# One row maximum per component and a fixed bank order in differential-attention scores

## The chip, the cores and the metric

The kernel runs on one core of a Trainium2 chip. The metric is device time in microseconds (us), the median over runs. The core's engines run side by side, each with its own instruction stream in a fixed order, and wait for each other through semaphores: PE (TensorE, matmuls and transposes; PEld is its weight load), DVE (VectorE), ACT (ScalarE), POOL (GpSimd) and SP (SyncE), which issues the DMA transfers. PE writes its results to PSUM, which has eight banks of 512 float32 columns on each of 128 partitions.

## What is computed

One layer of a hybrid block over 1024 latent tokens and 256 context tokens, width 1024. A modulated RMSNorm and one wide input projection feed two branches, a gated linear attention and a differential attention; each passes its own projection, they are merged through sigmoid gates, and one output projection follows. The change lies in the differential attention. Each of its 8 heads has two components, with one softmax each over 256 + 1024 keys:

```python
def one_block(qs):
    qb1, qb2 = qs
    s1 = jnp.einsum('bhqd,bhkd->bhqk', qb1, k1).astype(jnp.float32) * scale
    s2 = jnp.einsum('bhqd,bhkd->bhqk', qb2, k2).astype(jnp.float32) * scale
    a = jax.nn.softmax(s1, axis=-1) - lam * jax.nn.softmax(s2, axis=-1)
    return jnp.einsum('bhqk,bhkv->bhqv', a.astype(v.dtype), v)
```

## The kernel before

The program has a first part (norms, projections, gated linear attention), the attention stretch, and a last part (branch and output projections). The attention works in 64 units, one for each head and block of 128 queries.

In a unit the scores of both components, 2 x 1280 columns, fill one PSUM tile `s5` of five banks (0 to 4). Component 0 has columns 0 to 1279, component 1 columns 1280 to 2559, so both share bank 2: the last 256 columns of component 0 (its tail) and the first 256 of component 1 (its tail). `att_scores` issues for component 0 four matmuls of 512 columns (two key chunks, each with two accumulating halves), then the four tail matmuls of both components, then the four of component 1. `att_max` takes three negated row maxima on DVE: over component 0's 1024 columns, over both tails at once (128 x 2), over component 1's 1024. `att_exp` combines a component's maximum with its tail's by a small DVE minimum, and takes the exponential of all 1280 columns on ACT with that bias and a running sum. `att_mix` forms the difference of the two softmaxes (up to a factor) on DVE. `att_tr` transposes it in ten pieces on PE, `att_split` splits each into two float32r parts on ACT, POOL and DVE, `att_av` multiplies by the values for two units together, and `att_fin` normalises and stores the result.

Three counters, `s0`, `s1` and `st`, guard the scores: `s0` and `s1` a component's main columns, given back after its exponential; `st` both tails, given back after the second exponential of the unit. `banked` adds the semaphore waits between engines that use the same bank, in whichever direction they are issued, and takes away those between different banks. `att_keys` loads the keys of a head into slots of the tile `hk`, three of them (tag `kk`), two for each head; a head's event `ev_k` is set when both of its components are there, and both slots are given back after the head's last scores.

PE has other work to do in between: `fill` computes gate projections (kind 0) and the branch projections (kinds 1 and 2) in half tiles of 24 matmuls, at the lowest priority. While the scores' PSUM pools are open these write the tile `mb`, afterwards one of five tiles `mc`. When a kind ends, its input buffers `h0` and `h1` are loaded anew (`h<-d_aT`, `h<-d_bT`).

The order of all instructions is made when the program is built: `Driver` keeps a planned time for each engine (`op`, with `LAT` as the delay from one engine to the next), tasks are generators that yield the event or planned time they wait for, and the due task with the best priority goes next. `Driver.key` says which pieces of a tile count as one in that plan. So a change in one task can move every other task's instructions.

Of the kernel before, what the change touches and what calls it, by code (L numbers as in the profile page):

```python
# [11 lines left out]
F32R = mybir.dt.float32r  # L12
BF16 = mybir.dt.bfloat16
AF = mybir.ActivationFunctionType
ALU = mybir.AluOpType
# [5 lines left out]
P = 128  # L21
# [3 lines left out]
T = S + CTX  # L25
# [33 lines left out]
class Driver:  # L59
# [43 lines left out]
    def op(self, eng, cost, outs, ins):  # L103

        t = self.now if eng == "PE" else self.free[eng]
        shared = list(outs) + [x for x in ins if x.space == PSUM]
        for x in ins:
            t = max(t, self.ready.get(self.key(x), 0.0))
        for x in shared:

            end, by = self.last.get(self.key(x), (0.0, eng))
            t = max(t, end if by == eng else end + self.LAT[by])
        for x in outs:
            if eng != "PE":
# [6 lines left out]
        for x in ins + list(outs):  # L121
# [107 lines left out]
class Hybrid:  # L229
# [1 line left out]
    TAGS = dict(  # L231
        h0=("sb", 16), h1=("sb", 16), raw=("sb", 3), sm=("sb", 48),

        hk=("sbK", 1), hc=("sbK", 16), kk=("sbK", 3),

        w=("sbA", 18), p=("sbA", 5), pl=("sbA", 4), rope=("sbA", 1),

# [8 lines left out]
        e5=("sbB", 6), at4=("sbB", 6), at2=("sbB", 2), ac=("sbB", 2), b1k=("sbB", 5), fin=(None, 2),  # L246
# [4 lines left out]
        mb=("psW", 1), s0=("psB", 1), s1=("psB", 1), st=("psB", 1), s5=("psB", 1), b1=("psB1", 2), mc=("psC", 5), mz=("psD", 2),  # L251
# [93 lines left out]
    def banked(self, ins, eng, *banks):  # L345


        seen, info = set(), mybir.DependencyInfo(mybir.DependencyClass.Sync, mybir.DependencyReason.DATA)
        for prev, by, on in reversed(self.recent):
            if by == eng:  # L350
                continue
            if on.isdisjoint(banks):
                self.tc.declare_no_dep(ins, prev, reason="other banks")
            elif by not in seen:
                seen.add(by)
                self.tc.add_manual_dep(ins, prev.name, info, reason="the same bank")
        self.recent = self.recent[-48:] + [(ins, eng, set(banks))]
# [1369 lines left out]
    def att_keys(self):  # L1727

        for hd in range(8):
            c, x = hd // 4, hd % 4  # L1730
            for i in range(10):
                yield self.ev_st["dk", c, i]
            if hd:
                yield self.ev_q[0, 1]
            else:
                yield self.gla_free[3]
                yield from self.acq("hc", 16)
                Driver.places = (T, 2 * T, 3 * T)
                self.hk = self.t("hk", [P, HK], F32R)
            K = []  # L1740
            for comp in range(2):
                rows = slice(64 * comp, 64 * comp + 64)
                yield from self.acq("kk")
                m = (2 * hd + comp) % 3
                kt = self.hk[:, m * T:(m + 1) * T]
                self.dma(kt[0:64], self.d_kT[0][c][x, rows])
                self.dma(kt[64:128], self.d_kT[1][c][x, rows])
                K.append(kt)
            self.K[hd] = K
            self.d.set(self.ev_k[hd], self.d.when(*K))  # L1750

    def att_queries(self):
        yield self.ev_b2
# [30 lines left out]
    def att_scores(self):  # L1784

        nc, d = self.nc, self.d
        yield self.ev_b
        s5 = self.t("s5", [P, 2 * T])
        for hd in range(8):
            for qt in range(8):  # L1790
                pr, qs = qt // 2, slice((qt % 2) * P, (qt % 2) * P + P)
                yield self.ev_k[hd]
                yield self.ev_q[hd, pr]
                K, Q = self.K[hd], self.Q[hd, pr]

                def score(po, comp, o, n):
                    bank = po.offset % (2 * T) // 512
                    for j in range(2):
                        e = self.mm(po, Q[comp][:, j, qs], K[comp][:, o:o + n], j == 0, j == 1)
                        self.banked(self.ins, "PE", bank)  # L1800
                    return e

                u = dict(hd=hd, qt=qt, E=[None, None], mt=self.t("sm", [P, 2]), mx=[self.t("sm", [P, 1]) for _ in range(2)],
                         z=self.t("sm", [P, 2]), left=2, ev=[Event() for _ in range(3)])

                for comp in range(2):
                    yield from self.acq(f"s{comp}")
                    pm = s5[:, 1536 * comp:1536 * comp + 1024]
                    for x, (o, n) in enumerate(self.MAIN[comp]):
                        e = score(pm[:, x * 512:(x + 1) * 512], comp, o, n)  # L1810
                        if x == 0:
                            yield AtPE(0)
                    d.spawn(self.att_max(u["ev"][comp], u["mx"][comp], pm, 3 * comp, 3 * comp + 1), On(e, "DVE"), prio=-3)
                    yield AtPE(0)
                    if comp == 0:
                        yield from self.acq("st")
# [4 lines left out]
                    elif qt == 7:  # L1821
                        self.rel("kk", e, 2)
# [6 lines left out]
    def att_max(self, ev, mx, pm, *banks):  # L1829
        self.dve.tensor_reduce(mx, pm, AX.X, ALU.max, negate=True)  # L1830
        self.banked(self.dve.ins, "DVE", *banks)
        self.d.set(ev)
        return
        yield

    def att_exp(self, u, comp, s5):
        d, mx = self.d, u["mx"][comp]
# [7 lines left out]
        e = self.act.activation(E, s5[:, 1280 * comp:1280 * comp + T], AF.Exp, bias=mx, accum_out=u["z"][:, comp:comp + 1])  # L1845
        self.banked(self.act.ins, "ACT", *range(2 * comp, 2 * comp + 3))
        self.rel(f"s{comp}", e)
        u["left"] -= 1
        if u["left"] == 0:
            self.rel("st", e)  # L1850
# [318 lines left out]
    def phase_b(self):  # L2169
        d = self.d  # L2170
# [14 lines left out]
            d.set(self.ev_b)  # L2185

        d.spawn(to_b(), prio=-3)
        self.ev_k, self.ev_v = [Event() for _ in range(8)], [Event() for _ in range(8)]
# [34 lines left out]
    def phase_c(self):  # L2223
        a, d = self.a, self.d
# [4 lines left out]

        def to_c():  # L2230
            yield self.ev_s2
            yield from self.idle("s0", "s1", "st")
            self.close("psB")
            self.open("psC")
            d.set(self.ev_c)
# [228 lines left out]
```

## Time and profile before

| | |
|---|---|
| runs | 1683.67, 1685.21, 1689.54 us; median 1685.21 |
| profiled execution, first to last instruction | 1685.9 us |
| DVE, ACT, POOL busy | 69%, 47%, 36% of the span |
| DMA moved | 302.84 MB, mean 180 GB/s |

The page lists of the profiled execution only the span; the runs are other executions of the same program. A group's row reads: line, engine, operation, tiles (out<-in), shapes and count, then busy us, mean ns of one, and the engine's idle time before these with what ended it. A row of busy times by stretch reads: start and end, length, then for PE, PEld, DVE, ACT and POOL the busy us with the count in brackets, then granted clock, DMA share and GB/s. All compute instructions stand at a line of a helper, so groups are told apart by their tiles: `s` is the score tile, `sm` small statistics, `e` the exponentials, `at` the split transposes, `b` the two banks for transposes and value products, `mb` and `mc` the fill.

### The profile page before, as it was taken

The numbers are of one execution on the slowest core, as the hardware profiler recorded it, in microseconds if no ns is written. First come the engines' busy times: TensorE is split into PE (matmuls) and PEld (weight loads), VectorE is DVE, ScalarE is ACT, GpSimd is POOL, SyncE is SP. The second block draws the span as 40 slices with busy tenths as digits, with TensorE's granted clock in tenths as the row PEclk, the third lists the DMA queues.
The fourth block names the chain that finished last, engine by engine and source line by source line (L and its number), as shares of the span: only waits on it lengthen the run. The fifth ranks groups of instructions, "written<-read, shape, count | busy, mean of one in ns | idle before, by whom it ended". The sixth has DMA issues, their size and how long they took to land.

```text
span 1685.9 us, 24403 instructions
## 1 busy us (share of the span) xinstructions
PE 1641.8 (97%) x8389; PEld 1358.3 (81%) x8389; DVE 1167.5 (69%) x2035; ACT 788.4 (47%) x1624; POOL 601.7 (36%) x649
## 2 busy tenths in 40 slices
PE   8999999999999999999999999999999999999999
PEld 3788788888788888888878888888888787887887
DVE  4797853455578697687762988787787887525694
ACT  4666423343334535455442665556666555411231
POOL 1500200000156475465530446555565555700000
PEclk9999999999999999999999999999999999999999
DMA  8557947687683665645375344345368552279422
GB/s 305 167 205 258 325 164 248 226 282 273 200 258 114 197 203 169 207 134 169 117 196 154 85 128 132 104 116 138 113 169 245 167 157 67 98 234 337 151 100 75
DMA packets 255884, 302.84 MB, mean 180 GB/s; under 512 B 21480, under 2 KB 173968, under 8 KB 255760
## 3 DMA queue, kind: packets, MB, share of 16 engines
q1 hardware_dynamic: 255760, 301.29, 56.9%
q8 instruction: 66, 1.08, 0.3%
q14 instruction: 58, 0.48, 0.1%
HBM read 203.71 MB, written 97.52 MB: 179 GB/s over the span
## 4 chain that ended last, share of the span: by engine, by line
PE 43%; DVE 6%; ACT 2%; DMA 2%; POOL 2%; issue 2%; ACTq 0%; DVEq 0%; POOLq 0%; SPq 0%
PE mc L335 10%; PE mm L335 7%; PE mb L335 7%; PE s L335 6%; PE b L335 5%; DVE sm L197 3%; PE b L361 3%; POOL at L197 2%; DVE e L197 2%; PE go L335 1%; ACT e L197 1%; DMA h<-d_bT 1%; PE mz L335 1%; PE gs L335 1%; PE tp L361 1%
## 5 line engine op out<-in xcount | busy, mean ns | idle before, releaser
L335 PE MATMUL mm<-w,h 128*128 128x512 f32 x1260 | 319.3, 402 | 0.6 <-DVE w L197 0.4
L335 PEld LDWEIGHTS mm<-w,h 128*128 128x128 f32 x1260 | 232.0, 189 | 48.0 <-issue 1.0
L197 DVE TENSOR_REDUCE sm<-s 128x1 f32<-128x1024 f32 (+1 forms) x192 | 194.4, 1037 | 49.0 <-PE s L335 47.4
L335 PE MATMUL mb<-h,wt 128*128 128x512 f32 x744 | 204.5, 407 | 2.5 <-ACT ft L197 2.1
L197 ACT ACTIVATE e<-s,sm 128x1280 f32<-128x1280 f32 x128 | 169.9, 1330 | 68.0 <-DVE sm L197 60.3
L197 POOL TENSOR_TENSOR at<-ac,at 128x512 fp32r<-128x512 f32 x128 | 184.7, 1443 | 10.7
L197 POOL TENSOR_SCALAR at<-ac 128x512 fp32r<-128x512 f32 x128 | 100.6, 786 | 236.0 <-ACT ac L197 166.9
L335 PE MATMUL s<-hk,aq 128*128 128x512 f32 (+1 forms) x768 | 178.2, 365 | 3.2 <-ACT e L197 1.1
L335 PEld LDWEIGHTS mb<-h,wt 128*128 128x128 f32 x744 | 131.1, 190 | 25.9 <-ACT ft L197 3.6
L335 PE MATMUL mc<-h,wt 128*128 128x512 f32 x600 | 141.2, 392 | 1.7 <-DMA h<-d_bT 0.8
L335 PE MATMUL mm<-h,w 128*128 128x512 f32 x576 | 139.4, 398 | 2.7 <-ACT p L197 1.1
L335 PEld LDWEIGHTS s<-hk,aq 128*128 128x128 f32 x768 | 122.3, 190 | 23.9 <-ACT e L197 5.1
L335 PEld LDWEIGHTS mc<-h,wt 128*128 128x128 f32 x600 | 111.3, 188 | 26.9 <-DMA h<-d_bT 3.3
L335 PE MATMUL b<-at,vv 128*128 128x256 f32 x960 | 130.6, 285 | 0.5 <-POOL at L197 0.4
L335 PEld LDWEIGHTS mm<-h,w 128*128 128x128 f32 x576 | 108.6, 191 | 27.0 <-DVE h L197 1.4
L335 PEld LDWEIGHTS b<-at,vv 128*128 128x128 f32 x960 | 122.7, 190 | 5.6 <-POOL at L197 1.2
L197 POOL TENSOR_TENSOR sm<-sm,nhalf 128x2 f32<-128x2 f32 (+2 forms) x94 | 106.1, 1129 | 53.6 <-DVE sm L197 48.1
L197 DVE TENSOR_TENSOR w<-raw,w 128x512 fp32r<-128x512 f32 x120 | 92.5, 789 | 31.5 <-ACT w L197 30.3
L197 ACT ACTIVATE ac<-b 128x512 f32<-128x512 f32 x120 | 71.1, 600 | 84.9 <-PE b L361 79.7
L197 DVE SCALAR_TENSOR_TENSOR e<-e,sm,e 128x1280 f32<-128x1280 f32 x64 | 108.7, 1698 | 0.6
L197 ACT ACTIVATE w<-raw 128x512 fp32r<-128x512 f32 x120 | 72.5, 628 | 70.3 <-DVE raw L197 22.8
L361 PE MATMUL b<-ident,e 128*128 128x128 f32 x598 | 92.5, 276 | 12.4 <-DVE at L197 4.3
(283 smaller groups left out, 2832.5 us busy)
## 6 DMA issues: line engine op xcount, KB each, us to landing
raw<-in_w_in SPq DMA_DIRECT2D x63, 512.0 KB, 4.7
g<-d_s SPq DMA_DIRECT2D x32, 640.0 KB, 5.2
aq<-d_qT SPq DMA_DIRECT2D x128, 128.0 KB, 3.4
d_dv<-pl SPq DMA_DIRECT2D x40, 256.0 KB, 2.2
gv<-d_v SPq DMA_DIRECT2D x40, 256.0 KB, 3.2
d_kT<-pl SPq DMA_DIRECT2D x40, 256.0 KB, 3.0
hk<-d_kT SPq DMA_DIRECT2D x32, 320.0 KB, 5.7
vv<-d_dv SPq DMA_DIRECT2D x16, 640.0 KB, 6.2
```

Of the source, the lines that this page charges most:

```text
L197: self.ins = f(out, *args, **kw).ins
L335: self.ins = self.nc.tensor.matmul(out, lhsT, rhs, start=start, stop=stop, skip_group_check=more).ins
L361: self.nc.tensor.transpose(out, src, self.ident[:n, :n])
```

## The change

`att_max` goes. Per component there is one maximum over its 1280 columns, in `att_exp`. The tail of component 0 is issued ahead of its main columns, the tail of component 1 behind its own and only after the first maximum. Two gates per unit fix the order on bank 2: the first exponential is issued after the second tail, the second exponential after the next unit's first tail. The counter `st` is gone. `banked` no longer adds waits between ACT and DVE. The plan's `op` treats the score banks one by one, and in them makes PE follow ACT and DVE, and ACT and DVE follow PE, but not each other. Keys have a fourth slot, a tile of its own (`kx`), and an event for each component.

```diff
@@ Driver
-        if x.name.startswith("s5"):
-            o = ap.offset % (2 * T) if ap is not x else 0
-            return x.name + ("t" if ap.free_size() <= 512 and o // 512 == 2 else "ab"[o >= 1280])
+    @staticmethod
+    def banks(ap):
+        x = getattr(ap, "tensor", ap)
+        if not x.name.startswith("s5"):
+            return ()
+        o = ap.offset % (2 * T) if ap is not x else 0
+        return [f"{x.name}b{b}" for b in range(o // 512, (o + ap.free_size() - 1) // 512 + 1)]
@@ Driver.op
+        scores = [b for x in list(outs) + list(ins) for b in self.banks(x)]
+        if scores:
+            outs, ins = ([x for x in xs if not self.banks(x)] for xs in (outs, ins))
+            for b in scores:
+                for by in ("ACT", "DVE") if eng == "PE" else ("PE",):
+                    t = max(t, self.last.get((b, by), -1.0) + self.LAT[by])
...
+        for b in scores:
+            self.last[b, eng] = end
@@ banked
-            if by == eng:
+            if by == eng or "PE" not in (by, eng):
                 continue
@@ att_keys
-                m = (2 * hd + comp) % 3
-                kt = self.hk[:, m * T:(m + 1) * T]
+                m = (2 * hd + comp) % 4
+                if m == 3 and hd == 1:
+                    yield self.ev_b
+                    self.kx = self.t("kx", [P, T], F32R)
+                kt = self.hk[:, m * T:(m + 1) * T] if m < 3 else self.kx
...
-            self.d.set(self.ev_k[hd], self.d.when(*K))
+                self.d.set(self.ev_k[hd, comp], self.d.when(kt))
@@ att_scores
                 for comp in range(2):
+                    yield self.ev_k[hd, comp]
                     yield from self.acq(f"s{comp}")
+                    if comp == 0:
+                        score(s5[:, 1024:1280], 0, *self.TAIL[0])
+                        if last:
+                            d.set(last["gate"][1])
+                        last = u
                     pm = s5[:, 1536 * comp:1536 * comp + 1024]
                     for x, (o, n) in enumerate(self.MAIN[comp]):
                         e = score(pm[:, x * 512:(x + 1) * 512], comp, o, n)
                         if x == 0:
                             yield AtPE(0)
-                    d.spawn(self.att_max(u["ev"][comp], u["mx"][comp], pm, 3 * comp, 3 * comp + 1), On(e, "DVE"), prio=-3)
-                    yield AtPE(0)
-                    if comp == 0:
-                        yield from self.acq("st")
-                        pt = s5[:, 1024:1536].rearrange("p (c k) -> p c k", c=2)
-                        for x in range(2):
-                            e = score(pt[:, x], x, *self.TAIL[x])
-                        d.spawn(self.att_max(u["ev"][2], u["mt"], pt, 2), On(e, "DVE"), prio=-3)
+                    if comp == 1:
+                        yield u["ev"][0]
+                        yield d.whenpe(u["mx"][0])
+                        e = score(s5[:, 1280:1536], 1, *self.TAIL[1])
+                        d.set(u["gate"][0])
...
+                    if qt == 7:
+                        self.rel("kk", e)
@@ att_exp
-        yield u["ev"][2]
-        yield u["ev"][comp]
-        yield d.on("DVE", mx)
-        self.dve.tensor_scalar(mx, mx, u["mt"][:, comp:comp + 1], None, ALU.min)
+        pm, banks = s5[:, 1280 * comp:1280 * comp + T], range(2 * comp, 2 * comp + 3)
+        self.dve.tensor_reduce(mx, pm, AX.X, ALU.max, negate=True)
+        self.banked(self.dve.ins, "DVE", *banks)
+        d.set(u["ev"][comp])
         yield from self.acq("e5")
         E = u["E"][comp] = self.t("e5", [P, T])
+        yield u["gate"][comp]
         yield d.on("ACT", mx)
```

More of the change, by code (lines that the diff above doesn't have):

```diff
@@ L120, in op @@
             self.free[eng] = end
-        for x in ins + list(outs):
+        for b in scores:
+            self.last[b, eng] = end
+        for x in list(ins) + list(outs):
             k = self.key(x)
@@ L1788, in att_scores @@
         s5 = self.t("s5", [P, 2 * T])
+        last = None
         for hd in range(8):
@@ L1798, in score @@
                     for j in range(2):
-                        e = self.mm(po, Q[comp][:, j, qs], K[comp][:, o:o + n], j == 0, j == 1)
+                        e = self.mm(po, Q[comp][:, j, qs], self.K[hd, comp][:, o:o + n], j == 0, j == 1)
                         self.banked(self.ins, "PE", bank)
                     return e
-                u = dict(hd=hd, qt=qt, E=[None, None], mt=self.t("sm", [P, 2]), mx=[self.t("sm", [P, 1]) for _ in range(2)],
-                         z=self.t("sm", [P, 2]), left=2, ev=[Event() for _ in range(3)])
+                u = dict(hd=hd, qt=qt, E=[None, None], mx=[self.t("sm", [P, 1]) for _ in range(2)],
+                         z=self.t("sm", [P, 2]), left=2, ev=[Event() for _ in range(2)], gate=[Event(), Event()])
                 for comp in range(2):
+                    yield self.ev_k[hd, comp]
                     yield from self.acq(f"s{comp}")
+                    if comp == 0:
[3 more added lines that the diff above has]
+                        last = u
                     pm = s5[:, 1536 * comp:1536 * comp + 1024]
@@ L1812, in att_scores @@
                             yield AtPE(0)
[L1813 to L1822 removed]
+                    if comp == 1:
[3 more added lines that the diff above has]
+                        d.set(u["gate"][0])
+                        if (hd, qt) == (7, 7):
+                            d.set(u["gate"][1])
+                    if qt == 7:
+                        self.rel("kk", e)
                     d.spawn(self.att_exp(u, comp, s5), On(e, "DVE"), prio=-3)
@@ L1827, in att_scores, with att_exp @@
                 d.set(self.ev_u[8 * hd + qt])
-    def att_max(self, ev, mx, pm, *banks):
+    def att_exp(self, u, comp, s5):
+        d, mx = self.d, u["mx"][comp]
+        pm, banks = s5[:, 1280 * comp:1280 * comp + T], range(2 * comp, 2 * comp + 3)
         self.dve.tensor_reduce(mx, pm, AX.X, ALU.max, negate=True)
         self.banked(self.dve.ins, "DVE", *banks)
[L1832 to L1837, printed above, removed]
-        yield u["ev"][2]
-        yield u["ev"][comp]
-        yield d.on("DVE", mx)
-        self.dve.tensor_scalar(mx, mx, u["mt"][:, comp:comp + 1], None, ALU.min)
+        d.set(u["ev"][comp])
         yield from self.acq("e5")
         E = u["E"][comp] = self.t("e5", [P, T])
+        yield u["gate"][comp]
         yield d.on("ACT", mx)
-        e = self.act.activation(E, s5[:, 1280 * comp:1280 * comp + T], AF.Exp, bias=mx, accum_out=u["z"][:, comp:comp + 1])
-        self.banked(self.act.ins, "ACT", *range(2 * comp, 2 * comp + 3))
+        e = self.act.activation(E, pm, AF.Exp, bias=mx, accum_out=u["z"][:, comp:comp + 1])
+        self.banked(self.act.ins, "ACT", *banks)
         self.rel(f"s{comp}", e)
@@ L2187, in phase_b @@
         d.spawn(to_b(), prio=-3)
-        self.ev_k, self.ev_v = [Event() for _ in range(8)], [Event() for _ in range(8)]
+        self.ev_k, self.ev_v = {(hd, comp): Event() for hd in range(8) for comp in range(2)}, [Event() for _ in range(8)]
         for g in (self.att_keys, self.att_queries, self.att_values):
@@ L2231, in to_c @@
             yield self.ev_s2
-            yield from self.idle("s0", "s1", "st")
+            yield from self.idle("s0", "s1")
             self.close("psB")
```

14 lines of the change are left out of this document (5 added, 9 removed).

## The prediction

> **What bounds the kernel now.** I read, in this order, the view of spans and clocks, the page's busy times, and a table of busy time cut at the starts of heads 0, 8, 16 … of the 64 (head, query tile) units, which I call heads 0 to 7 (eight units each).
>
> ```profile
> core 0: 1685.9 us, clock 0.994
> ```
> ```profile
> PE 1641.8 (97%) x8389; PEld 1358.3 (81%) x8389; DVE 1167.5 (69%) x2035; ACT 788.4 (47%) x1624; POOL 601.7 (36%) x649
> ```
> ```profile
> 911.30:967.70 56.40, 55.52 (x306) 46.00 (x307) 46.05 (x75) 32.89 (x58) 24.34 (x21) 1.00 0.29 83
> 967.70:1029.10 61.40, 59.47 (x353) 50.04 (x353) 53.02 (x103) 39.15 (x81) 29.79 (x28) 1.00 0.48 129
> 1029.10:1099.20 70.10, 67.76 (x409) 58.02 (x408) 56.10 (x105) 41.36 (x85) 39.20 (x36) 1.00 0.43 122
> 1099.20:1169.70 70.50, 68.82 (x417) 58.69 (x416) 53.85 (x105) 41.31 (x86) 38.57 (x36) 1.00 0.46 123
> 1169.70:1236.30 66.60, 66.60 (x409) 57.48 (x408) 53.94 (x105) 40.65 (x83) 39.69 (x37) 1.00 0.42 119
> 1236.30:1303.00 66.70, 66.70 (x409) 57.60 (x409) 54.50 (x107) 41.51 (x88) 41.53 (x36) 1.00 0.75 220
> 1303.00:1375.00 72.00, 66.78 (x399) 57.05 (x399) 56.94 (x109) 40.21 (x86) 34.26 (x36) 0.98 0.59 171
> 1375.00:1438.60 63.60, 57.18 (x346) 48.58 (x345) 51.06 (x101) 36.46 (x77) 38.13 (x36) 0.97 0.28 85
> 1438.60:1685.90 247.30, 241.91 (x1142) 199.93 (x1140) 140.05 (x233) 61.03 (x114) 27.11 (x27) 1.00 0.51 168
> ```
>
> PE is busy almost throughout, so the time is PE's work plus PE's gaps. The table shows where: the scores run from 911.3 to 1438.6 us, 527.3 us for 64 units, 8.24 us each; then 247.3 us follow. "Busy" counts a matmul until its end, though the next one starts earlier, so I take the cost of one matmul from runs of them in the chain of waits (start us, length us, what):
>
> ```profile
> 1192.56 2.15 PE b L335 x18
> ...
> 1293.86 0.93 PE s L335 x4
> ...
> 1310.97 1.38 PE mb L335 x6
> ...
> 1313.97 1.41 PE s L335 x8
> ...
> 1316.80 0.44 PE b L361 x4
> ...
> 1534.68 82.35 PE mc L335 x362
> ```
>
> So a 512-column score matmul is 0.233 us (0.93/4), a 256-column one 0.12 (the eight are four of each: (1.41-0.93)/4), a value matmul 0.119, a transpose 0.11, a fill matmul 0.231 during the scores and 0.2275 after them (82.35/362). I counted each kind in the built instruction order between the first and the last score matmul, for both kernels. Before, heads 0 to 7 hold 48.4, 58.2, 65.5, 66.8, 67.9, 64.1, 62.5 and 61.0 us of PE work, 494.4 in all. Against the durations above, PE's stalls are 8.0, 3.2, 4.6, 3.7, -1.3, 2.6, 9.5 and 2.6 us: **32.9 us**, 0.51 per unit. That is all that a change of order can win here.
>
> What the stalls are, shown at the worst one and at the two places where the clock fell (first the order of time, then busy times as above; the fraction behind the POOL column is the granted clock):
>
> ```profile
> 1339.98 2.94 DVE L197 TENSOR_REDUCE sm<-s 128x1 f32<-128x1024 f32 x3
> ...
> 1343.52 1.06 PE L361 MATMUL b<-ident,e 128*128 128x128 f32 x8 [3.35 <-DVE sm L197]
> ```
> ```profile
> 1340.00:1344.00 4.00, 0.65 (x6) 0.51 (x6) 4.00 (x11) 0.86 (x1) 0.00 (x0) 1.00 0.00 0
> 1344.00:1348.00 4.00, 3.98 (x17) 3.23 (x16) 2.48 (x6) 2.59 (x6) 3.32 (x5) 0.60 0.33 112
> ...
> 1408.00:1412.00 4.00, 2.31 (x6) 1.78 (x7) 3.13 (x10) 3.35 (x8) 0.12 (x1) 0.70 0.54 185
> ```
> ```profile
> 1409.69 0.66 PE L361 MATMUL b<-ident,e 128*128 128x128 f32 x2 [2.03 <-DVE b1k L197]
> ```
>
> VectorE works through three maxima in a row, the two instructions that would free a PSUM bank for the transposes stand behind them, and PE idles 3.35 us. Then the clock is 0.60 for 4 us, which costs 0.40 x 4 = 1.6 us more. In a sentence of its own: the Trainium skill, "TensorE: Matmul & The Clock Gate", Part 1, says that an idle window of about 3.4 us halves the clock for at least as long; by it only gaps that long would pay the 1.6 us, but the 0.70 above followed a wait of 2.03 us, so the measured row decides and shorter gaps can pay it too.
>
> **The change part by part.**
>
> ```profile
> L197 ACT ACTIVATE e<-s,sm 128x1280 f32<-128x1280 f32 x128 | 169.9, 1330 | 68.0 <-DVE sm L197 60.3 <-DVE e L197 5.8 <-PE b L361 1.4
> L197 DVE TENSOR_REDUCE sm<-s 128x1 f32<-128x1024 f32 x128 | 155.6, 1216 | 48.4 <-PE s L335 46.8 <-ACT e L197 1.3 <-PE b L361 0.3
> ...
> L197 DVE SCALAR_TENSOR_TENSOR e<-e,sm,e 128x1280 f32<-128x1280 f32 x64 | 108.7, 1698 | 0.6
> ...
> L197 DVE TENSOR_REDUCE sm<-s 128x2 f32<-128x512 f32 x64 | 43.6, 681 | 0.6 <-PE s L335 0.6
> ...
> L197 DVE TENSOR_SCALAR sm<-sm,sm 128x1 f32<-128x1 f32 x192 | 34.3, 205 | 1.6
> ```
>
> *Maxima.* The 64 tail maxima (43.6 us) and the 128 small minima (128 x 0.205 = 26.2 us) go. The 128 maxima grow from 1024 to 1280 columns. That form is not in the trace; from 1.216 us at 1024 and 0.681 at 512 a column costs 1.045 ns, so 1.483 us each, 34.2 us more in all. Bounds: no longer than now (0), or 1.216 x 1280/1024 = 1.52 us (38.9 us). VectorE gains 43.6 + 26.2 - 34.2 = 35.6 us, 4.45 per head. It is not the engine that ends the time, so this pays only where PE waits for VectorE.
>
> *Fill work moves.* Score, value and transpose counts stay; in the built order 150 fill matmuls leave the stretch of the scores and stand behind it (720 before, 570 after). So heads 0 to 7 hold 41.5, 50.4, 58.9, 63.7, 61.2, 60.0, 64.4 and 59.8 us, **459.7 us** in all, and the tail grows by 150 x 0.2275 = **34.1 us**. Total PE work is the same to 0.6 us. So everything hangs on the stalls: under 33.5 us in 64 units and the kernel is faster.
>
> *The new hand-offs.* Three waits per unit now sit in PE's own order: the second component's tail matmuls wait for the first maximum (they write the bank it reads); the next unit's first tail waits for the first exponential; the next unit's second component waits for the second exponential, which itself waits for that first tail. Behind each of them on PE stand transposes, value and fill matmuls that need not wait, and behind those ScalarE's copies. What a hand-off needs comes from the order of time:
>
> ```profile
> 1184.65 1.33 ACT L197 ACTIVATE e<-s,sm 128x1280 f32<-128x1280 f32 x1
> ...
> 1185.88 0.19 ACT L197 ACTIVATION_READ_ACCUMULATOR e<-s,sm 128x1 f32 x1
> ...
> 1186.12 0.81 PEld L335 LDWEIGHTS s<-hk,aq 128*128 128x128 f32 x4
> ...
> 1186.29 1.07 PE L335 MATMUL s<-hk,aq 128*128 128x512 f32 x4
> ...
> 1194.55 1.09 PE L335 MATMUL s<-hk,aq 128*128 128x512 f32 x4
> ...
> 1195.75 1.23 DVE L197 TENSOR_REDUCE sm<-s 128x1 f32<-128x1024 f32 x1 [0.19 <-PE s L335]
> ```
>
> Exponential to matmul: 1186.29 - 1184.65 = 1.64 us. Matmul to reader: 1195.75 - 1194.55 less the 0.93 of issue = 0.27. So PE needs 1.91 us of other work across an exponential, and 0.27 + 1.48 + 0.22 = 1.97 across a maximum (0.22 as from the accumulator's end, 1186.07, to the matmul). The built order puts between them, in the median, 2.36 us (maximum), 3.18 (first exponential) and 2.36 (second). It is short in 3, 9 and 11 units, by 2.2, 2.6 and 1.1 us in all, 5.9 us; 3.4 of it lie in heads 2 to 7. That holds if VectorE and ScalarE are free in time. In the new order the 1.7 us mix never stands ahead of a first maximum, and ahead of the second in 63 of 64 units, so the tightest wait has only small work before it. Bounds for the three together: nothing, to the worst head of the trace on all units, 9.5/8 = 1.19 us each, 76 us. I take the shortages, and add stalls of the usual kind below.
>
> *Four key buffers, split key event.* The chain shows the one key load that held anything:
>
> ```profile
> 1296.21 8.32 DMA hk<-d_kT
> 1304.55 5.20 DMA b1k<-d_dg
> ```
>
> It lies in head 5, whose whole stall is 2.6 us; so the fourth buffer wins at most that once, and I give it no term. It costs four transfers moved ahead on SP's queue past the gate and query loads, the same bytes.
>
> *Sum.* Heads 0 and 1 have less PE work than VectorE can follow: its busiest head ran at 53.02/61.40 = 0.8635, so they last (46.05-4.45)/0.8635 = 48.2 and (53.02-4.45)/0.8635 = 56.3 us, stalls of 6.7 and 5.9. For heads 2 to 7 I take the mean of the present heads 4, 5 and 7 (-1.3, 2.6, 2.6: 1.3 us), since head 6's fill, which uses VectorE per half tile, now stands behind the scores; 7.8 us. With the shortages: 6.7 + 5.9 + 7.8 + 3.4 = 23.8 us. Then 911.3 + 459.7 + 23.8 + 247.3 + 34.1 = **1676.2 us** on the scale of the profiled span, 1685.9. The median of the runs, 1685.21, is 0.7 below it, inside their spread, so I leave it: **1676**, 9.5 us or 0.6% faster.
>
> **The rivals.** *The clean schedule*: stalls like head 4's and 5's everywhere ((2.6-1.3)/16, 0.1 us per unit, 6 us in all): 1658. For it: both heads had VectorE at 0.81 and lost nothing. Against: PE's work per unit falls from 7.7 to 7.2 us, and all other engines must keep that pace.
>
> *The stall only changes its place*: VectorE falls by 7% in work, PE's stretch by 7% too, so PE outruns it as before; 0.5 us per unit stays: 911.3 + 459.7 + 32.9 + 281.4 = 1685. Here the change would do what it says and win nothing. For it: VectorE's share of PE's work, 425.5/494.4 (the eight rows' sum) = 0.86, becomes 389.9/459.7 = 0.85.
>
> *The hand-offs decide*: slower. Place: the second component's matmuls behind an exponential that waits for a tail, two crossings between PE and ScalarE. The cover is 2.36 against 1.91, so from 0.45 us of delay on ScalarE (one 0.6 us copy of transposes ahead of the exponential) every unit stalls. If such a copy is late in each unit, and half that (0.3 us) hits one of the other hand-offs, a unit loses 0.6 - 0.45 + 0.3 + 0.5 (as now) = 0.95 us, 61 us: 1713. Against: in the units that I followed in the order that copy stands early enough.
>
> *The fill's reload is exposed*: the gate projections end with the last scores, so the next fill's inputs load there.
>
> ```profile
> 1290.23 3.44 SPq L300 DMA_DIRECT2D h<-d_aT  x7
> ...
> 1307.17 4.52 SPq L300 DMA_DIRECT2D h<-d_aT  x9
> ```
>
> These are the second half of 32 loads, issued over 21.5 us (1290.23 to 1311.69) among others. In the new order the first half is issued from unit 57 on, some 50 us of PE work ahead; the second follows the last score, with 20.8 us of attention work (108 x 0.119 + 72 x 0.11) and 11 us of fill (48 x 0.2275) to cover it. If the 16 loads take twice as long, 12 us show: 1688.
>
> **How the numbers follow.** A run of this kernel tells about 0.3%, 5 us, from no change. Chances: the forecast 0.47 (own range 1665 to 1685), the clean schedule 0.12, the stall that changes place 0.18, the hand-offs 0.15, the reload 0.08. Faster (under 1680.2) is most of the first and all of the second: 0.36 + 0.12 + 0.08 of the rest's lower edges = 0.56; slower (over 1690.3) 0.15 + 0.03 + 0.04 = 0.22; the rest 0.22. The range runs from 1656, just under the clean schedule, to 1700, half way to the hand-offs' price; I leave some 0.07 below and 0.12 above.
>
> **What would show it.** Right: heads 2 to 7 last 60 to 66 us, heads 0 and 1 near 48 and 56; maxima of 1.48 us, 128 of them; VectorE some 35 us less busy; the last score near 1395; no clock of 0.5 between it and the first score. Wrong: PE's weight loads for the scores waiting tens of microseconds for ScalarE or the maxima; a gap of over 3 us after the last score on an input load; heads longer than now minus the moved fill.

## The result, and the profile after

| | before | after |
|---|---|---|
| median of the runs | 1686.1 us (1683.67 to 1689.54, 4 runs) | 1785.23 us (1781.1 to 1786.83, 4 runs) |
| profiled execution | 1685.9 us | 1779.4 us |

The ratio is 1.0579 (95% interval 1.0557 to 1.06): slower by 99 us, where 1676 had been forecast. Three of the four runs of before are those of the table ahead; the fourth took 1686.99 us.

The page of after, busy times and the groups that answer to those of before (line 209 is the helper that was line 197, 347 was 335; of PE's score matmuls the row of the page holds the 576 that read keys from `hk`):

```profile
PE 1666.7 (94%) x8389; PEld 1364.7 (77%) x8389; DVE 1152.5 (65%) x1843; ACT 792.2 (45%) x1624; POOL 597.4 (34%) x649
...
L209 DVE TENSOR_REDUCE sm<-s 128x1 f32<-128x1280 f32 x128 | 190.3, 1487 | 145.5 <-ACT e L209 80.5
...
L209 ACT ACTIVATE e<-s,sm 128x1280 f32<-128x1280 f32 x128 | 170.4, 1331 | 139.0 <-DVE sm L209 102.6
L347 PE MATMUL s<-hk,aq 128*128 128x512 f32 (+1 forms) x576 | 151.5, 391 | 64.3 <-ACT e L209 46.7
...
L347 PE MATMUL mc<-h,wt 128*128 128x512 f32 x744 | 170.8, 390 | 0.8 <-DVE wt L209 0.5
...
L347 PE MATMUL mb<-h,wt 128*128 128x512 f32 x600 | 166.3, 407 | 0.1
```

The other 192 score matmuls read the new slot `kx`; their row in the groups' view of after, and then the one row that before has for all 768:

```profile
L347 PE MATMUL s<-kx,aq 128*128 128x512 f32 (+1 forms) x192 | 48.8, 380 | 7.3 <-ACT e L209 6.8 <-DVE sm L209 0.3
```
```profile
L335 PE MATMUL s<-hk,aq 128*128 128x512 f32 (+1 forms) x768 | 178.2, 365 | 3.2 <-ACT e L197 1.1 <-ACT p L197 0.7 <-DMA hk<-d_kT 0.7
```

No engine became the bound: every engine's share of the span fell. What rose is waiting, in both directions between two engines. The exponentials on ACT were idle 139.0 us before they could start, 102.6 of it behind DVE's statistics (before: 60.3); the maxima on DVE 145.5 us, 80.5 of it behind the exponentials (before: 1.3); and PE's score matmuls, which had waited 1.1 us for exponentials, now wait 46.7 + 6.8 = 53.5.

The busy times by stretch, cut at the first score of heads 0 to 7 and at the last score:

```profile
906.30:965.80 59.50, 47.89 (x254) 38.32 (x254) 42.32 (x49) 30.36 (x52) 22.13 (x21) 0.97 0.30 83
965.80:1032.60 66.80, 58.11 (x328) 48.38 (x329) 47.90 (x71) 36.80 (x73) 29.06 (x28) 0.95 0.40 108
1032.60:1111.60 79.00, 65.57 (x379) 54.83 (x377) 52.58 (x81) 40.49 (x84) 38.88 (x36) 0.94 0.36 99
1111.60:1191.90 80.30, 68.16 (x397) 55.10 (x397) 50.85 (x81) 41.01 (x85) 38.35 (x36) 1.00 0.35 97
1191.90:1269.40 77.50, 68.53 (x393) 56.44 (x393) 52.86 (x85) 42.44 (x88) 36.95 (x36) 0.96 0.41 111
1269.40:1346.10 76.70, 65.89 (x386) 54.23 (x387) 52.92 (x81) 41.50 (x86) 39.76 (x36) 0.98 0.39 105
1346.10:1424.60 78.50, 68.90 (x400) 56.94 (x401) 51.38 (x82) 41.94 (x86) 40.11 (x36) 0.98 0.33 95
1424.60:1497.20 72.60, 61.92 (x355) 50.52 (x356) 50.37 (x77) 38.96 (x82) 35.59 (x34) 0.98 0.49 157
1497.20:1779.40 282.20, 274.58 (x1293) 228.45 (x1291) 148.72 (x240) 64.24 (x117) 26.44 (x26) 1.00 0.52 172
```

The last row is 282.2 us, where 247.3 + 34.1 = 281.4 had been forecast. The whole loss lies in the stretch of the scores: 590.9 us, against 527.3 before and 459.7 + 23.8 = 483.5 forecast. PE's work there is 459.7 us, so its stalls are 131.2 us, 2.05 per unit (0.51 before; a lower clock counts as a stall here). They lie in every head alike (14.8 to 20.2 us, with the work of each head counted in the built order), although DVE is busy for no more than 63 to 72% of a head.

One unit shows what the stalls are. The order of time of after, around units 39 and 40 (the first score of unit 40 starts head 5):

```profile
1266.29 1.48 DVE L209 TENSOR_REDUCE sm<-s 128x1 f32<-128x1280 f32 x1
...
1267.87 1.33 ACT L209 ACTIVATE e<-s,sm 128x1280 f32<-128x1280 f32 x1 [1.12 <-DVE sm L209]
...
1269.34 0.97 PE L347 MATMUL s<-hk,aq 128*128 128x256 f32 x4 [0.97 <-ACT e L209]
...
1269.88 1.33 ACT L209 ACTIVATE e<-s,sm 128x1280 f32<-128x1280 f32 x1
...
1271.33 1.49 DVE L209 TENSOR_REDUCE sm<-s 128x1 f32<-128x1280 f32 x1 [1.04 <-ACT e L209]
...
1273.24 2.50 DVE L209 SCALAR_TENSOR_TENSOR e<-e,sm,e 128x1280 f32<-128x1280 f32 x1
...
1275.66 1.48 DVE L209 TENSOR_REDUCE sm<-s 128x1 f32<-128x1280 f32 x1
...
1277.23 1.33 ACT L209 ACTIVATE e<-s,sm 128x1280 f32<-128x1280 f32 x1 [2.69 <-DVE sm L209]
...
1278.70 1.43 PE L347 MATMUL s<-hk,aq 128*128 128x256 f32 x6 [1.90 <-ACT e L209]
...
1279.24 1.33 ACT L209 ACTIVATE e<-s,sm 128x1280 f32<-128x1280 f32 x1 [0.32 <-PE s L347]
...
1280.69 1.49 DVE L209 TENSOR_REDUCE sm<-s 128x1 f32<-128x1280 f32 x1 [1.07 <-ACT e L209]
```

Read it as a closed loop, from one first exponential (1267.87) to the next (1277.23), each step counted from start to start. After the exponential the next unit's first tail on PE (1.47 us later), then the second exponential (0.54), then the next unit's first maximum (1.45), two small instructions and the mix of the former unit (1.91), the second maximum (2.42), and the next first exponential (1.57): 9.36 us, every step behind the one before it. The step to look at is the last: the maximum that this exponential needs had ended at 1272.82 (1271.33 + 1.49). It starts 4.41 us later, right behind the *other* component's maximum, which ends at 1277.14. And the first maximum at 1271.33 starts right behind the former unit's second exponential (1269.88 + 1.33 = 1271.21), of whose columns it reads none.

The two share one thing, bank 2. Component 0's maximum now reads banks 0, 1 and 2, component 1's banks 2, 3 and 4, and each exponential three banks as before, so any maximum meets any exponential in bank 2. In the built program the accesses of one bank by different engines are ordered whatever `banked` does, reads included: the layer that places the semaphores does it, and what `banked` contributed between ACT and DVE was to take such waits away where the banks differ. The edit in `banked` therefore took no wait away. A program with that one line put back, built and not run, has the same order on PE, DVE and ACT and the same waits. In the built program 52 of the 64 first exponentials carry a wait for their own unit's second maximum. Summed over the trace, a maximum and an exponential overlap in time for 18.6 us before and for 0.0 us after (from the starts and ends of all 128 of each).

The Trainium skill, "PSUM — Partial Sum Buffer", section "PSUM bank collisions raise a hardware error", says that the chip doesn't arbitrate between two engines in one bank, and that a dependency belongs between any two of them there, ScalarE against VectorE and read against read too. The 0.0 us agrees with such an order; no run here shows a collision.

### The profile page after: what moved, and what is told of

Same layout as the page of the kernel before. It is cut to its first block, busy times and chain, and to the rows that moved or that the text cites. A ratio compares the mean times of both kernels' runs of the same rounds, so it can differ in the third digit from the quotient of the medians.

```text
span 1779.4 us, 24229 instructions
## 1 busy us (share of the span) xinstructions
PE 1666.7 (94%) x8389; PEld 1364.7 (77%) x8389; DVE 1152.5 (65%) x1843; ACT 792.2 (45%) x1624; POOL 597.4 (34%) x649
## 4 chain that ended last, share of the span: by engine, by line
PE 34%; DVE 14%; ACT 5%; issue 4%; DMA 2%; POOL 1%; SPq 0%; ACTq 0%; DVEq 0%; POOLq 0%
PE mc L347 12%; DVE sm L209 9%; PE mm L347 7%; PE s L347 5%; DVE e L209 4%; ACT e L209 4%; PE b L347 3%; PE mb L347 2%; PE b L373 1%; PE go L347 1%; DMA b1k<-d_dg 1%; DVE b1k L209 1%; PE mz L347 1%; PE gs L347 1%; PE tp L373 1%
## 5 line engine op out<-in xcount | busy, mean ns | idle before, releaser
L209 DVE TENSOR_REDUCE sm<-s 128x1 f32<-128x1280 f32 x128 | 190.3, 1487 | 145.5 <-ACT e L209 80.5
L209 ACT ACTIVATE e<-s,sm 128x1280 f32<-128x1280 f32 x128 | 170.4, 1331 | 139.0 <-DVE sm L209 102.6
L347 PE MATMUL s<-hk,aq 128*128 128x512 f32 (+1 forms) x576 | 151.5, 391 | 64.3 <-ACT e L209 46.7
L209 POOL TENSOR_TENSOR at<-ac,at 128x512 fp32r<-128x512 f32 x128 | 193.3, 1510 | 10.7
L347 PE MATMUL mc<-h,wt 128*128 128x512 f32 x744 | 170.8, 390 | 0.8 <-DVE wt L209 0.5
L347 PEld LDWEIGHTS s<-hk,aq 128*128 128x128 f32 x576 | 93.9, 198 | 98.3 <-ACT e L209 64.5
L347 PE MATMUL mb<-h,wt 128*128 128x512 f32 x600 | 166.3, 407 | 0.1
L347 PEld LDWEIGHTS mc<-h,wt 128*128 128x128 f32 x744 | 139.1, 188 | 30.2 <-DVE wt L209 1.0
L347 PE MATMUL b<-at,vv 128*128 128x256 f32 x960 | 138.8, 292 | 5.6 <-DVE at L209 2.3
L347 PEld LDWEIGHTS mb<-h,wt 128*128 128x128 f32 x600 | 104.8, 190 | 16.8 <-ACT ft L209 0.9
L209 ACT ACTIVATE p<-mm 128x512 f32<-128x512 f32 (+1 forms) x104 | 59.9, 586 | 87.7 <-PE mm L347 79.0
```

The costliest lines, as they stand in the source:

```text
L209: self.ins = f(out, *args, **kw).ins
L347: self.ins = self.nc.tensor.matmul(out, lhsT, rhs, start=start, stop=stop, skip_group_check=more).ins
```

## The experiments

I held three theories. Theory 1: ACT and DVE take strict turns on bank 2, and the turns set the pace. Theory 2: PE's own new order (tail ahead, gates, second tail behind the first maximum) does it, the prediction's hand-offs. Theory 3: the turns would cost little if the plan, whose `op` was told that ACT and DVE don't follow each other, had known of them.

**Twins with and without the turns.** Two kernels that differ only in the waits between ACT and DVE: the order of all compute instructions is the same in both, and 20 of the 1009 transfers change places. The gates and the place of the mix are those of the change. Not all of its order is: the plan knows of the shorter maxima, and 36 more fill matmuls stand behind the scores (534 among them, 570 in the change). The maxima read only the 1024 columns in the component's own banks, so that they share no bank with the other component's exponential, and in the second twin the waits stay as if they did. Of the two added calls of `banked` the one with `own=own` is the first twin's, the one with `own=None` the second's.

```diff
+    def banked(self, ins, eng, *banks, own=None):
...
-            if by == eng or "PE" not in (by, eng):
+            if by == eng:
                 continue
-            if on.isdisjoint(banks):
+            a, b = (on, banks) if "PE" in (by, eng) else (mine, own or banks)
+            if a.isdisjoint(b):
                 self.tc.declare_no_dep(ins, prev, reason="other banks")
...
+        own = range(3 * comp, 3 * comp + 2)
-        self.dve.tensor_reduce(mx, pm, AX.X, ALU.max, negate=True)
-        self.banked(self.dve.ins, "DVE", *banks)
+        self.dve.tensor_reduce(mx, s5[:, 1536 * comp:1536 * comp + 1024], AX.X, ALU.max, negate=True)
+        self.banked(self.dve.ins, "DVE", *banks, own=own)
+        self.banked(self.dve.ins, "DVE", *banks, own=None)
...
-        e = self.act.activation(E, pm, AF.Exp, ...)
+        e = self.act.activation(E, pm, AF.Tanh, ...)
```

> Both this kernel and its twin take each maximum over the 1024 columns of a component's own two banks (its 256 tail columns are left out of the maximum) and use tanh in place of the exponential, so the output is not the reference's. The order of all instructions is the same in the two; here ACT and DVE, which now read different banks, do not wait for each other. Theory 1 (the two engines take turns on the shared bank 2, one after the other, and that is where the 100 us went): 1690 us (1660 to 1715). Theory 2 (PE's own new hand-offs, tail behind maximum and exponential behind tail, cost it): within 15 us of the twin, both 1740 to 1780.

> The twin: same instructions in the same order, maxima over 1024 columns, but ACT and DVE still wait for each other as if the maximum read the shared bank. Theory 1: 1785 less at most 128 x 0.27 us for the shorter maxima, 1740 to 1780, and 50 us or more over its twin. Theory 2: the same time, but the twin has it too.

Without the waits 1687.31 us (ratio 1.0, 0.9987 to 1.0013), with them 1769.01 (1.048, 1.0462 to 1.0498): the waits alone cost 81.7 us, at the same instructions on every compute engine, in the same order. Of it 78.2 us lie in the stretch of the scores (489.8 and 568.0 us in the profiles). Groups of the first twin, then of the second:

```profile
L209 ACT ACTIVATE e<-s,sm 128x1280 f32<-128x1280 f32 x128 | 170.4, 1331 | 39.7 <-PE s L347 32.6 <-DVE e L209 6.8
...
L209 DVE TENSOR_REDUCE sm<-s 128x1 f32<-128x1024 f32 x128 | 156.1, 1219 | 95.9 <-PE s L347 95.9
```
```profile
L209 ACT ACTIVATE e<-s,sm 128x1280 f32<-128x1280 f32 x128 | 170.3, 1331 | 129.0 <-DVE sm L209 100.8 <-PE s L347 25.9 <-DVE at L209 1.3
...
L209 DVE TENSOR_REDUCE sm<-s 128x1 f32<-128x1024 f32 x128 | 156.1, 1219 | 142.2 <-PE s L347 73.7 <-ACT e L209 67.6 <-PE b L374 0.9
```

The busy us and the mean durations agree; the idle us behind the other engine (100.8 and 67.6) vanish in the first twin. The fill moves with the plan and not with the waits, so it is the same in both. The windows view of the first twin, heads 0, 1, 2 and 7:

```profile
906.30:956.80 50.50, 44.54 (x257) 37.04 (x257) 36.77 (x50) 30.40 (x53) 23.38 (x21) 1.00 0.27 79
956.80:1012.80 56.00, 51.99 (x315) 44.55 (x316) 46.95 (x74) 37.35 (x73) 31.02 (x27) 1.00 0.50 138
1012.80:1078.00 65.20, 61.48 (x386) 53.28 (x386) 48.53 (x82) 40.31 (x84) 36.29 (x37) 1.00 0.42 116
...
1337.30:1396.10 58.80, 56.91 (x354) 49.02 (x353) 45.16 (x78) 37.73 (x80) 36.64 (x35) 1.00 0.48 152
```

These heads come near those that the prediction describes (48 and 56 us, then 60 to 66; last score near 1395): it forecast, in the main, a kernel without the turns. That kernel is no faster than before, though its maxima are even shorter (1.219 us) than those of the change. With 36 fill matmuls fewer it has 459.7 - 36 x 0.231 = 451.4 us of PE work in its 489.8 us of scores, so its stalls are 38.4 us, where 23.8 had been forecast and before has 32.9.

Theory 1 holds for the bulk of the loss. The waits also bring the granted clock down: over the scores it is 1.00 in the first twin and 0.97 in the second. That belongs to their price and was not separated from it; the missing 0.03 of 568.0 us make 17 us at most (an estimate, as if PE had work at every moment).

**The old order of PE.** The changed kernel with PE's score matmuls in the order of before (main columns, both tails, main columns), `st` back and the gates gone; one maximum over 1280 columns stays.

```diff
-                    if comp == 0:
-                        score(s5[:, 1024:1280], 0, *self.TAIL[0])
...
-                        yield d.whenpe(u["mx"][0])
-                        e = score(s5[:, 1280:1536], 1, *self.TAIL[1])
...
+                    if comp == 0:
+                        yield self.ev_k[hd, 1]
+                        yield from self.acq("st")
+                        for x in range(2):
+                            e = score(s5[:, 1024 + 256 * x:1280 + 256 * x], x, *self.TAIL[x])
...
-        yield u["gate"][comp]
...
+            self.rel("st", e)
```

> The changed kernel with one maximum per component over 1280 columns, but the score matmuls in the order of before (main columns of component 0, both tails, main columns of component 1; counter st back; no gates). Theory 1 (bank 2 is read by every maximum and every exponential, whatever the order of the matmuls): still far slower than before, 1740 to 1800. Theory 2 (the fixed order on PE): the hand-offs are gone, so within 1.5% of before, 1665 to 1710.

1732.44 us (1.027, 1.0254 to 1.0286), just under theory 1's interval and far over theory 2's. Half of the loss remains with no new hand-off on PE, and half goes, for which theory 1 as I held it has no place. This run doesn't show that PE's order alone took that half away, since the plan moved the mix along with it: in the change the mix of a unit stands between the next unit's two maxima in 63 units, here ahead of both in 62 (counted in the built programs).

**A plan that knows the turns.**

```diff
-                for by in ("ACT", "DVE") if eng == "PE" else ("PE",):
+                for by in [x for x in ("PE", "ACT", "DVE") if x != eng]:
```

> The changed kernel, with a plan that knows that ACT and DVE wait for each other on the score banks; the waits themselves stay. Theory 1 (the two engines take turns, whatever the plan knows): a chain of two maxima, two exponentials, a mix and two matmul hops per unit stays, 8.9 us or more, so 1730 to 1790. Theory 3 (the waits are harmless once the plan orders the other work around them): 1665 to 1705.

1734.58 us (1.0288, 1.0253 to 1.0323): theory 3 falls as the whole cause, but one line of the plan is worth 51 us. The waits view from 905 to 1510 us, first of after, then of this kernel:

```profile
ACT e L209 <- DVE sm L209: 102.6, 69, 5.2
DVE sm L209 <- ACT e L209: 96.6, 56, 4.4
...
PE s L347 <- ACT e L209: 53.5, 50, 4.4
...
PE s L347 <- DVE sm L209: 16.4, 15, 2.1
```
```profile
DVE sm L209 <- ACT e L209: 90.7, 54, 4.3
ACT e L209 <- DVE sm L209: 59.8, 38, 5.2
...
PE s L347 <- DVE sm L209: 36.5, 29, 2.8
...
PE s L347 <- ACT e L209: 12.1, 9, 2.5
```

The turns are still there (columns: us in total, times, longest); PE has found other work for most of the waits for an exponential, and waits longer for maxima.

**Two ways to shorten the loop, on top of that plan.** First the mix of a unit, which in the kernel with that plan stands between the next unit's two maxima in 61 units, put behind both; then instead the first exponential put ahead of its unit's second maximum, which is the turn that the timeline above showed.

```diff
+                self.units.append(u)
...
+        n = 8 * u["hd"] + u["qt"] + 1
+        if n < 64:
+            yield self.units[n]["ev"][1]
```

> The same, and the mix of a unit is issued behind the next unit's second maximum instead of between its two maxima. Theory 1: the mix (0.16 + 0.27 + 1.7 us) leaves the chain of turns and runs while ACT has the bank, so some 1.5 us less per unit than the plan-aware kernel, 60 us or more under it: 1670 to 1710. Theory 3: within 15 us of the plan-aware kernel.

1703.72 us (1.009, 1.0062 to 1.0119): 31 us less than with the plan alone. The direction is theory 1's and the time lies in its interval, though the gain is half of what was expected.

```diff
...
+        if comp:
+            yield u["x0"]
         self.dve.tensor_reduce(mx, pm, AX.X, ALU.max, negate=True)
...
+        if comp == 0:
+            d.set(u["x0"])
```

> The plan-aware kernel with the first exponential issued ahead of the second maximum, so that it doesn't wait for the second component. Theory 1: the mix runs while ACT has the bank, as with the late mix, so 1670 to 1715; the number of turns is the same. Theory 3: within 15 us of the plan-aware kernel.

1773.65 us (1.0512, 1.0485 to 1.0538): a miss, 39 us *slower* than the plan alone. The order of time shows where the time went:

```profile
1271.06 1.54 DVE L209 SCALAR_TENSOR_TENSOR e<-e,sm,e 128x1280 f32<-128x1280 f32 x1
...
1272.85 1.47 DVE L209 TENSOR_REDUCE sm<-s 128x1 f32<-128x1280 f32 x1
...
1274.38 1.65 PE L347 MATMUL s<-hk,aq 128*128 128x256 f32 x4 [3.71 <-DVE sm L209]
```

Component 0's next tail is written to bank 2 as well, so with the second maximum now behind the exponential that tail waits for the maximum, and the mix stands ahead of this maximum. Over the stretch of the scores, from the waits view:

```profile
PE s L347 <- DVE sm L209: 76.0, 64, 3.7
...
PE s L347 <- ACT e L209: 0.7, 2, 0.4
```

The turn was not removed but handed to PE, which can least afford it. Its plan also put fewer fill matmuls between the scores; the groups' view of the kernel with the plan alone, then of this one:

```profile
L347 PE MATMUL mb<-h,wt 128*128 128x512 f32 x672 | 185.4, 406 | 0.5 <-DVE ft L209 0.5
```
```profile
L347 PE MATMUL mb<-h,wt 128*128 128x512 f32 x480 | 136.9, 412 | 1.4 <-ACT ft L209 1.3
```

So although its last score comes 15.0 us earlier (at 1459.4, against 1474.4), 192 x 0.2275 = 43.7 us more follow it: 28.7 us, and the two profiled spans differ by 27.4 (1767.3 and 1739.9). A stretch of scores that ends sooner says nothing as long as the fill in it isn't counted.

**Both remedies together.** After those two results I formed theory 4, that with the old order the plan's knowledge would add nothing, and set it against theory 1 with PE's order as an added turn.

```diff
-                for by in ("ACT", "DVE") if eng == "PE" else ("PE",):
+                for by in [x for x in ("PE", "ACT", "DVE") if x != eng]:
...
```

> The order of the score matmuls of before (main columns of component 0, both tails, main columns of component 1; st lock back, no gates), one maximum over 1280 columns per component, and a plan that knows that VectorE and ScalarE wait for each other on the score banks. Two kernels next to it stand at 1732.4 us (same order, plan ignorant) and 1734.6 us (gated order, plan aware). Theory 1 (turns cost what the plan doesn't see, and the gated order adds a turn of PE's to them): both remedies together do better than either, 1695 to 1720 us. Theory 4 (with the old order the st lock already keeps the plan honest, and what is left is the price of the turns themselves): 1725 to 1740 us, no better than either. PE's waits for exponentials at score matmuls: theory 1 under 10 us, theory 4 about as in the ignorant one, 32 us.

1693.38 us (1.0044, 1.0026 to 1.0062), just under theory 1's interval; theory 4 falls. Its waits, in the same window as those above:

```profile
ACT e L209 <- DVE sm L209: 125.5, 63, 5.1
DVE sm L209 <- ACT e L209: 67.7, 53, 3.3
...
PE s L347 <- ACT e L209: 10.1, 13, 2.4
```

ACT and DVE wait for each other about as much as in after (193 us against 199), and PE waits 10.1 us for exponentials in place of 53.5. The four kernels together:

| ratio to before | plan doesn't know the turns | plan knows them |
|---|---|---|
| order of the change | 1.0579 (after) | 1.0288 |
| order of before | 1.027 | 1.0044 |

By the medians each remedy is worth 51 and 53 us alone, and 92 us together. The second row differs from the first in more than PE's order: in both of its kernels the plan puts the mix ahead of both maxima (in 62 and 60 of 63 units). With the mix behind both maxima and the order of the change, the plan that knows took 1703.72 us, 10.3 more than both remedies. So what PE's hand-offs cost by themselves may be far less than the 41 us between the rows; no run separates them.

**The keys alone.** The kernel before with the fourth slot and one event for each component, and nothing else of the change.

```diff
-                m = (2 * hd + comp) % 3
-                kt = self.hk[:, m * T:(m + 1) * T]
+                m = (2 * hd + comp) % 4
...
+                kt = self.hk[:, m * T:(m + 1) * T] if m < 3 else self.kx
...
-            self.d.set(self.ev_k[hd], self.d.when(*K))
+                self.d.set(self.ev_k[hd, comp], self.d.when(kt))
```

> The kernel before with four key slots and an event for each component, nothing else. Theories 1 and 2: the key load held PE about 1 us in one place, so 0 to 0.4% under before: 1678 to 1688.

1678.86 us (0.9947, 0.993 to 0.9964), in the interval expected and under both kernels, by half a per cent. Against it, one maximum per component at its best (order of before, plan that knows) costs 14.5 us. It has the turns, but the plan's order differs too, so how much of the 14.5 us are the turns was not shown.

**One small minimum in place of two.** On top of the keys, a single 128 x 2 minimum combines the maxima of both components with the tails'.

```diff
-        self.dve.tensor_scalar(mx, mx, u["mt"][:, comp:comp + 1], None, ALU.min)
...
+            for ev in u["ev"]:
+                yield ev
+            self.dve.tensor_tensor(mx, mx, u["mt"], ALU.min)
```

> The kernel before with four key slots, and one small minimum for both components in place of two. 64 x 0.2 us less on DVE, which ends nothing: 0 to 0.3% under the kernel with four slots alone, 1674 to 1681. If the first exponential then waits longer for the second component's maximum than it does now, over 1685.

1696.05 us (1.0056, 1.0034 to 1.0077), 17 us slower than the keys alone, as the second case of the expectation has it. The first exponential now needs the second maximum, the dependency of the change in small, this time through data: from the first score to the last the exponentials wait 85.2 us for statistics, 65.4 with the keys alone. The plan's order moved with the edit (780 fill matmuls among the scores, 729 with the keys alone), so the 17 us are not all shown to be this wait.

## Why the prediction was wrong, point by point

- *What bounds the kernel*: right. The end is PE's work plus PE's stalls; the work came out as counted, and the tail after the last score came out at 282.2 us for 281.4.
- *Maxima*: right. They last 1.487 us for 1.483, and the three groups fall from 155.6 + 43.6 + 26.2 to 190.3, 35.1 us. DVE's busy total fell by only 15.0: the mixes and the scalings of `b1k` grew by 2.2 and 3.1 us, and the summed durations of all its instructions fell by 28.9 us, of which the busy total, that counts two overlapping ones once, shows 15.0. It decides nothing, as the prediction said of DVE.
- *Fill work moves*: right, 600 and 744 in the rows of `mb` and `mc`, which were 744 and 600.
- *The new hand-offs*: **the failed step.** The needs were sized well: from exponential to tail 1.47 us in the loop (1.64 taken). But the 5.9 us of shortage, of which 3.4 enter the sum, stood on the sentence "That holds if VectorE and ScalarE are free in time", and they were not. Each waited for the other on bank 2, and the stalls became 131.2 us in place of 23.8; the twins put 81.7 us on these waits. The prediction took the change at its word that ACT and DVE no longer wait for each other. One step decides it: list the banks that each reader covers. A maximum widened from 1024 to 1280 columns takes in bank 2, and with it the turn against all exponentials. The prediction even saw that the mix stands ahead of the second maximum in 63 units, and let it pass because the tightest wait, for the first maximum, has only small work before it; but through bank 2 the first exponential waits for the second maximum, and the next tail behind it. For that wait the loop has the mix and a maximum, 2.42 + 1.57 us, where the prediction priced none.
- *Stalls by head*: a wrong reading, apart from the turns. The sums 494.4 and 459.7 us come out of the built orders; their split by head doesn't. Head 0 of before has 306 matmuls in the prediction's own table. They are 96 of scores, 96 of fill, 60 of values and 54 transposes, 54.0 us at the prediction's prices, where it took 48.4. Counted so, heads 0 to 7 of before stall for 2.4, 4.0, 3.6, 3.1, 0.8, 0.9, 8.5 and 9.6 us: head 7 is the worst one, not a usual one. With heads 0 and 1 of the change at 43.4 and 52.0 us of work, the prediction's own rule (six heads at the mean of heads 4, 5 and 7) then gives 4.8 + 4.3 + 22.6 + 3.4 = 35.1 us of stalls and 1687.5 us, no gain. The first twin, without the turns, has 38.4 us.
- *The rivals*: "the hand-offs decide" had the sign and the place (PE's score matmuls behind an exponential, 53.5 us in 50 waits) with 0.15 chance. Its mechanism, a late copy on ScalarE, was another, and its 0.95 us per unit (the 0.5 of before among them) was less than half of the measured 2.05. *The stall only changes its place* is what the first twin shows, 1687.31 us for its 1685. That the change doesn't do what it says was read as a stall changing its place; the case that a wait said to be gone is still in the program was not considered, though the wait could be read off the built instructions.
- *Four key buffers*: mis-sized. No term was given, and the edit alone measures 0.53% (0.36 to 0.70), 8 us by the medians. The working looked only at the load in the chain, in head 5. The stretch of the scores fell from 527.3 to 519.9 us, while the score matmuls of before wait only 0.7 us for keys; the plan's order moved with the edit too. Which waits went was not separated.
- *Sum*: 911.3 + 459.7 + 23.8 + 281.4. Measured: 906.3 + 459.7 + 131.2 + 282.2 = 1779.4. The stalls are 107.4 us too small; the scores begin 5.0 earlier.

What stays open: how much of the 81.7 us, up to some 17, is the lower clock that waits bring; what PE's order costs apart from the place of the mix; why the mix behind both maxima gains 31 and not 60 us; and whether the scores of the two components can lie in banks of their own. The changed kernel with the waits on bank 2 taken away was not tried, since then both engines would read one bank with nothing to order them.

## What to carry to other kernels

Before an instruction is widened, list the PSUM banks that it covers and every reader of another engine on them: in this program a bank that is shared makes the two take turns although both only read, and the price here was 81.7 us for two engines that were 65% and 45% busy. A scheduler that plans without such a wait puts the wrong work around it; telling it was worth 51 us without a change to the kernel's work. Fewer or shorter instructions on an engine that isn't the bound won nothing here by themselves (the first twin), and lost where one that remains needs its inputs later (the single minimum).

## What the runs showed that was not expected

Two readers of one bank never overlapped (0.0 us in after, against 78.2 us in the first twin, where the banks differ). And the loss doesn't grow with the waits of ACT and DVE: with 199 us of them in after and 193 us in the kernel with both remedies, the times differ by 92 us. What goes with the time is how long PE stands behind them. Its score matmuls wait for exponentials and maxima 69.9 us in after, 50.0 in the second twin, 48.6 with the plan that knows, 32.1 with the old order, 29.3 with the late mix, 10.1 with both remedies and 3.7 in the first twin; the medians are 1785, 1769, 1735, 1732, 1704, 1693 and 1687 us. Only the kernel with the first exponential ahead stands out of the row (76.7 us, 1774).
